# The first feed-forward units of a hybrid decoder step: order of stores, fetches, copies, sums and splits

## The chip, the core and the metric

The kernel runs on one core of a Trainium2 chip. The core has a matrix engine (TensorE, PE in the profile, with its weight loads as PEld), a vector engine (VectorE, DVE), a scalar engine (ScalarE, ACT), GpSimd (POOL) and a sync engine (SyncE, SP) that here only issues DMAs. Each engine works through its own queue in order and waits on semaphores for the others. The metric is the device time of one execution in microseconds: 2213.25 us before the change, the median of three runs (2213.18 to 2215.95).

## What is computed

One inference step of one decoder layer, in float32, for a prompt of 2048 tokens and 64 sample tokens (8 sequences of 8), with a model width of 1024. The mixing half has sliding-window attention and gated linear attention side by side; the feed-forward half, in which the change lies, is this:

```python
mix = jnp.einsum('bte,ed->btd', jnp.concatenate([attn.astype(x.dtype), gla_out], axis=-1), w_out)
x = x + rms_norm(mix, g_mix_post)

h = rms_norm(x, g_ffn_pre)
u = jax.nn.relu(jnp.einsum('btd,df->btf', h, w_up))
f = jnp.einsum('btf,fd->btd', u * u, w_down)
x = x + rms_norm(f, g_ffn_post)
```

with `w_up` of 1024 x 4096 and `w_down` of 4096 x 1024.

## The kernel before

**Splitting into high and low parts.** To get float32 results from a faster format, every operand of a matmul is split in two: ScalarE writes the high part (a copy into `float32r`), VectorE writes the remainder (`source - high`). `split_by` (line 1555) is this pair. A product is then three matmuls per 128 rows of depth: high x high, high x low, low x high.

**Row blocks.** The 2048 tokens are 16 row blocks of 128, and the samples are one more. The output projection goes over them in `B_ORDER` (line 68), which ends with 14, 11, 15. For each row block `residual` (line 1474) adds the residual and normalizes, then eight transposes on TensorE write the result to two PSUM banks, ScalarE copies these into a tile `ht`, and for every second row block of a pair VectorE makes four differences in `ht` and a DMA stores the tile to DRAM, `h_d` (line 1514). `residual` is a generator: each `next` does one part, so that its parts can be placed between other work. `ht` has one slot for all pairs (tag `st` of the pool `keep`), so that a new pair's copies must wait until the store of the pair before has landed. Row block 14's store empties the slot for row block 11's copies. After them, row block 15's copies and its store use the same tile; unit two's result tile takes the slot over from there.

**Units.** The product with `w_up` is computed for each half of the prompt in 16 units of 256 columns (`up`, line 1652). A unit is one level of a Strassen-like scheme: seven products of 12 matmuls, numbered 1 to 7, each of an operand block `H[p]` (kept on chip, in two parts) and of a weight or a sum of weights. In the first half of the prompt there are also two products for the samples (numbered 0 and 8) and two transposes of their result (9). Products 1, 0 use the weight half `a` (`ua`, `ub` in the profile is the bank that a product fills, not the weight); 2, 8, 4 use the half `b` (called w1 here); 5, 7 use the sums `s13`; 6, 3 use the sums `s24`. VectorE makes the sums (`sums_13`, `sums_24`), ScalarE and VectorE split them (`split_sums`) and the weights (`split_up`). VectorE also gathers the products into seven results, ScalarE squares them, and a DMA stores them (`s_d`).

Products 2, 3 and 4 add to the bank that 1, 5 and 7 have filled, so that the earlier value must have been read by then. The bank of 5 and 3 is called Z, that of 7 and 4 V. `uc` is Z's name in the profile, `ud` that of V in unit one, `ua` that of product 6 in unit one and of products 1 and 2 in unit two. `sam` is the sample products' bank; ScalarE's copy of it (`both`) is what the two transposes read.

**Unit one** is special. Its blocks `H[3]` to `H[7]` come from `h_d` by DMA and are split while it runs: blocks 5 and 7 just ahead of it, 6, 3 and 4 within it. `UP_FIRST` (line 49) gives the order of its products: 1, 0, 2, 8, 5, 7, 9, 6, 3, 4. Behind each, `opening` (line 1771) places other work: the parts of row block 15's `residual` (`last_rows`), the blocks' splits, and the sums and splits for unit two. The instructions of this stretch on TensorE, ScalarE and VectorE (`te`, `ac`, `dv`) are chained by the class `InOrder` (line 120) in the order in which the program issues them. DMAs on SP, and row blocks 11 and 14, are ordered by a planner that simulates the program; `tc.issue_after` puts a DMA behind another on SP.

**Memory.** Block 6 comes into a temporary tile in memory that the output projection frees, blocks 3 and 4 into pools in memory that row block 15's tiles free. Blocks 3 and 4 are fetched into the place of their low part and split in place (`split_in_place`). Weights of odd units come into the staging tiles through which block 5 came (`hs_pool`). Down sums (`sum_down`, from unit three on) need pieces of `w_down` that `load_down` fetches into two tiles that held gains before.

Of the kernel before, what the change touches and what calls it, by code (L numbers as in the profile page):

```python
# [21 lines left out]
P = 128  # L22
# [118 lines left out]
def hybrid_step_kernel(ctx: ExitStack, tc: tile.TileContext, I, O):  # L141
# [1330 lines left out]
    gpost = gains(I["g_mix_post"][0], 0, "gpost")  # L1472

    def residual(i, banks, tensor=nc.tensor, scalar=nc.scalar, vector=nc.vector):

# [20 lines left out]
        for h in range(2):  # L1496
            kk = slice(h * 4, h * 4 + 4)
            pt = (bank([P, 512], "ce"[h], f"xnT_{i}_{h}") if te is tensor else next_bank("cdce", f"xnT_{i}_{h}")).rearrange("p (k t) -> p k t", k=4)
            for k in range(4):
                tensor.transpose(pt[:, k, :n], x1[:n, (h * 4 + k) * P : (h * 4 + k + 1) * P], ident[:n, :n])  # L1500
            if i == NB:
                split_copy(xsT[:, kk, :NS], xsT[:, kk, NS:], pt[:, :, :NS], vector)
                continue
            ht = sums[sb, j]
            scalar.activation(ht[:, (6, 2)[h] if second else h], pt, AF.Copy)
            if sb == 0 and not second:
                split_copy(H[h + 1][0][:, :, q], H[h + 1][1][:, :, q], pt, vector)
# [5 lines left out]
        kept = slice(2 * (sb == 0), 7)  # L1513
        nc.sync.dma_start(h_d[sb][:, kept, :, q], ht[:, kept])

    h_raws = {}

    def fetch_h(sb, p, home="h"):
        h_raws[p] = []
        for k in range(0, KT // 2, 2):  # L1520
            if isinstance(home, tuple):
                pool, tag = U[home[k // 2]], "s"
            else:
                pool, tag = {"h": hs_pool, "t": keep}.get(home) or U[home], f"{home}{k // 2}"
            raw = pool.tile([P, 2, BT], F32, tag=tag, name=f"hraw_{sb}_{p}_{k}", bufs=1)
            nc.sync.dma_start(raw, h_d[sb][:, p - 1, k : k + 2])
            h_raws[p].append(raw)

    def load_h(sb, p, scalar=nc.scalar, vector=nc.vector):
# [13 lines left out]
    def load_up(sb, fc):  # L1543
# [8 lines left out]
        for c, raw in enumerate(raws[sb, fc]):  # L1552
            nc.sync.dma_start(raw, src[:, 4 * c : 4 * c + 4])

# [14 lines left out]
    for n, i in enumerate(B_ORDER[2:]):  # L1569
# [25 lines left out]
    fetch_h(0, 7, ("s24h", "s24l"))  # L1595
    fetch_h(0, 6, "tmp")

# [54 lines left out]
    def up(sb, fc, before, steps=iter(())):  # L1652
# [6 lines left out]
        sam = bank([P, BT], "b", f"sam_{fc}") if sb == 0 else None  # L1659
        place = []  # L1660

# [58 lines left out]
        for p in UP_FIRST if first else UP_ORDER:  # L1720
# [37 lines left out]
        add(4, s(5), s(0))  # L1758
        if sb == 0:
            sample_features(fc, sam)  # L1760

# [9 lines left out]
    def opening(p, taken, ahead):  # L1771

        if p == 1:
            taken(p)
        elif p == 0:
            next(last_rows)
        elif p == 2:
            taken(p)
            next(last_rows)
            run(load_h(0, 6, ac, dv))  # L1780
            U.pop("tmp").release()
        elif p == 8:
            taken(p)
            sums_24(0, 0, dv)
            split_sums(0, 0, 24, ac, dv)
        elif p == 5:
            taken(p)
        elif p == 7:
            taken(p)
            next(last_rows)  # L1790
            close_pools(R)
            for q in H_LATE[3:]:
                h_pools[q] = open_pool(f"h_{q}")
            for q in H_LATE[:2:-1]:
                h_place(0, q)
                for k in range(0, KT // 2, 2):
                    loaded = nc.sync.dma_start(f32(H[q][1][:, k : k + 2]), h_d[0][:, q - 1, k : k + 2])
            with tc.issue_after(loaded.ins):
                load_up(0, 2)
        elif p == 9:  # L1800
            taken(p)
        elif p == 6:
            split_in_place(3)
            ahead("a")
            taken(p)
            split_in_place(4)
            run(last_rows)
            for half in range(2):
                load_down(0, half)
        elif p == 3:  # L1810
            ahead("s13")
            ahead("13")
        else:
# [12 lines left out]
    def sample_features(fc, sam):  # L1826
# [3 lines left out]
        ac.activation(sq, turned[:, :, 1], AF.Copy)  # L1830
        dv.tensor_tensor(sq, sq, turned[:, :, 0], op=ALU.add)
        squared(sq)
        split_by(ac, dv, parts[:, :, :NS], parts[:, :, NS:], sq)
# [252 lines left out]
    split_sums(0, 0, 13, ac, dv)  # L2086
    load_up(0, 1)
    next(last_rows)
    run(load_h(0, 7, ac, dv))
    for sb in range(NSB):  # L2090
# [13 lines left out]
        if sb == 0:  # L2104
            for p in (3, 4, 7, 6):
                h_pools.pop(p).release()
# [55 lines left out]
```

## Time and profile before

| | |
|---|---|
| median of 3 runs | 2213.25 us (2213.18 to 2215.95) |
| profiled execution | 2212.31 us |
| its span | 2210.4 us |
| TensorE granted clock, mean | 0.995 |
| HBM traffic | 266.34 MB read, 143.99 MB written |
| weight fetch of a unit (`raw`), issue to landing | 4.4 us for 512 KB |
| result store of a unit (`s_d`), issue to landing | 8.5 us for 1792 KB |

The profile is that of one execution. A row of it names the engine, the line, the operation and the tiles, written one first; most operations of this stretch go through `InOrder` and so show its line, L130, and are told apart by their tiles. Times are microseconds from the start of the span. An idle time is put down to what ended it: `[2.96 <-ACT s L130]` is 2.96 us of idle time that ended with ScalarE's write of a tile `s`. On `SPq` a row is the issue of a DMA, not its transfer. The first unit starts at 893 us and lasts some 30 us, of 2210.

### The profile page before, as it was taken

The page shows a single profiled execution, that of the slowest core. Times are in us where ns is not written, and L with a number is a line of the kernel's source. Part 1 is how long each engine was busy: PE and PEld are TensorE (multiplying, and loading weights), DVE is VectorE, ACT ScalarE, POOL GpSimd, SP SyncE. Part 2 cuts the span into 40 slices and gives each one's busy share as a digit, 9 for nine tenths or more (in the row PEclk, how much of TensorE's full clock was granted, in tenths as well). Part 3 has the DMA queues.
Part 4 walks back from the last instruction along what each step waited for, and adds up shares of the span by engine and source line. Part 5 has one row for each costly group of instructions (what it writes and reads, how often), then busy time and mean ns, then how long its engine had stood idle before and what let it go on. Part 6 is the DMA issues. An engine that isn't in the chain of part 4 may idle for free.

```text
span 2210.4 us, 34115 instructions
## 1 busy us (share of the span) xinstructions
PE 2166.2 (98%) x11784; PEld 1864.2 (84%) x11784; DVE 1530.4 (69%) x3101; ACT 1220.3 (55%) x2626; POOL 262.3 (12%) x418
## 2 busy tenths in 40 slices
PE   8999999999999999899999999999999999999998
PEld 7989989999997788688888887888888888888886
DVE  5888868777785665788888655547776666555566
ACT  5889867566664443555555544435455444454454
POOL 3576512111111010000000000000000000000000
PEclk9999999999999999999999999999999999999999
DMA  7344332224336665768777677768553344666685
GB/s 228 131 143 149 102 104 65 68 80 142 126 125 219 214 217 181 240 226 274 256 271 255 248 228 225 246 187 264 175 204 139 137 154 148 229 203 197 191 271 186
DMA packets 240185, 411.53 MB, mean 186 GB/s; under 512 B 25924, under 2 KB 142124, under 8 KB 235900
## 3 DMA queue, kind: packets, MB, share of 16 engines
q1 hardware_dynamic: 240012, 409.35, 55.8%
q8 instruction: 93, 1.52, 0.3%
q14 instruction: 80, 0.66, 0.1%
HBM read 266.34 MB, written 143.99 MB: 186 GB/s over the span
## 4 chain that ended last, share of the span: by engine, by line
PE 83%; DVE 7%; ACT 5%; DMA 2%; issue 2%; POOL 1%; SPq 0%; DVEq 0%; ACTq 0%; POOLq 0%
PE dn L130 27%; PE gproj L130 9%; PE uc L130 7%; PE ua L130 7%; PE out L1306 6%; PE proj L130 5%; PE ud L130 4%; PE ub L130 4%; PE ue L130 4%; PE sam L130 1%; PE dsam L130 1%; PE av L130 1%; PE o L130 1%; PE pT L130 1%; PE sc L130 1%
## 5 line engine op out<-in xcount | busy, mean ns | idle before, releaser
L130 PE MATMUL dn<-o0t,o0s 128*128 128x512 f32 x896 | 349.1, 390 | 1.7 <-ACT f L1936 1.5
L130 PE MATMUL dn<-o1t,o0s 128*128 128x512 f32 x896 | 349.5, 390 | 0.3 <-DVE o1t L219 0.2
L130 PE MATMUL dn<-o0t,o1s 128*128 128x512 f32 x896 | 349.3, 390 | 0.0
L219 DVE TENSOR_TENSOR o1s<-rs,o0s 128x512 fp32r<-128x512 f32 x224 | 154.6, 691 | 231.0 <-ACT o0s L218 224.8
L218 ACT ACTIVATE o0s<-rs 128x512 fp32r<-128x512 f32 x224 | 141.1, 631 | 306.2 <-PE dn L130 284.0
L130 PE MATMUL gproj<-wg,gxh 128*128 128x384 f32 x1024 | 272.4, 342 | 0.3 <-DVE gp_s L213 0.3
L130 ACT ACTIVATE st<-st 128x512 f32<-128x512 f32 x224 | 141.2, 630 | 141.8 <-DVE st L130 137.8
L130 PEld LDWEIGHTS dn<-o0t,o0s 128*128 128x128 f32 x896 | 168.2, 188 | 38.6 <-ACT f L1936 1.9
L130 PEld LDWEIGHTS dn<-o1t,o0s 128*128 128x128 f32 x896 | 168.2, 188 | 37.1 <-DVE o1t L219 1.1
L130 PEld LDWEIGHTS dn<-o0t,o1s 128*128 128x128 f32 x896 | 168.2, 188 | 35.4
L130 PE MATMUL uc<-H,s 128*128 128x512 f32 x768 | 188.5, 394 | 1.7 <-ACT s L130 1.2
L130 PEld LDWEIGHTS gproj<-wg,gxh 128*128 128x128 f32 x1024 | 183.8, 188 | 4.1 <-issue 3.1
L130 PE MATMUL gproj<-wg,gxl 128*128 128x384 f32 x576 | 186.0, 340 | 0.2 <-DVE gp_s L213 0.2
L130 PE MATMUL ua<-H,w 128*128 128x512 f32 x744 | 179.2, 390 | 0.0
L130 PEld LDWEIGHTS uc<-H,s 128*128 128x128 f32 x768 | 144.2, 189 | 33.2 <-ACT s L130 1.6
L130 PEld LDWEIGHTS ua<-H,w 128*128 128x128 f32 x744 | 139.7, 188 | 29.4
L1306 PE MATMUL out<-wo,mt 128*128 128x512 f32 x680 | 160.4, 394 | 2.6 <-ACT mt L218 1.5
L219 DVE TENSOR_TENSOR o1t<-rt,o0t 128x512 fp32r<-128x512 f32 x224 | 153.3, 684 | 6.7 <-ACT o0t L218 6.7
L208 POOL TENSOR_TENSOR frs<-rs_v,half 128x1 f32<-128x1 f32 (+1 forms) x13 | 10.1, 787 | 1213.5 <-DVE rs_v L206 693.1
L1306 PEld LDWEIGHTS out<-wo,mt 128*128 128x128 f32 x680 | 127.4, 189 | 29.6 <-ACT mt L218 1.9
L218 ACT ACTIVATE o0t<-rt 128x512 fp32r<-128x512 f32 x224 | 138.3, 618 | 6.7 <-PE dn L130 3.1
L130 DVE TENSOR_TENSOR st<-st 128x512 f32<-128x512 f32 x160 | 110.6, 691 | 26.9 <-ACT st L130 22.6
(398 smaller groups left out, 4318.0 us busy)
## 6 DMA issues: line engine op xcount, KB each, us to landing
s_d<-st SPq DMA_DIRECT2D x32, 1792.0 KB, 8.5
rs<-s_d SPq DMA_DIRECT2D x224, 256.0 KB, 3.0
raw<-in_w_up SPq DMA_DIRECT2D x64, 512.0 KB, 4.4
rt<-t_d SPq DMA_DIRECT2D x128, 256.0 KB, 3.9
rt<-in_w_down SPq DMA_DIRECT2D x96, 256.0 KB, 2.8
t<-in_w_down SPq DMA_DIRECT2D x64, 256.0 KB, 3.9
t_d<-t SPq DMA_DIRECT2D x32, 512.0 KB, 3.2
hraw<-h_d SPq DMA_DIRECT2D x20, 512.0 KB, 5.4
```

Of the source, the lines that this page charges most:

```text
L130: ins = call(*a, **k)
L208: nc.gpsimd.tensor_tensor(out, v[:n], e, op=ALU.pow)
L218: nc.scalar.activation(hi, src, AF.Copy)
L219: vector.tensor_tensor(lo, src, f32(hi), op=ALU.subtract)
L1306: te.matmul(banks[c], x, w[:, c * 512 : (c + 1) * 512], start=k + u == 0, stop=k == KT - 1 and u == len(products) - 1,)
```

## The change

Seven things in the stretch around unit one:

1. Row block 14's store is issued behind the fetches of block 6 and of unit two's weights, and those weights behind block 6.
2. Row block 11's copies out of the PSUM banks get a place in ScalarE's fixed order, behind product 2.
3. Block 3 is fetched, behind that store, into four free planes of unit one's result tile, and split from there. Block 4 alone is fetched into the place of its low part.
4. Row block 15's parts come one or two products earlier: its sums behind product 1, its transposes behind product 5 and not behind 7. The last part, differences and store, comes behind product 3 and not behind 6.
5. Block 7's split goes in two: the high parts ahead of unit one, the remainders behind product 1. The sums for `s24` come behind the sample product 0, their split ahead of block 6's.
6. The sums and splits for unit two are spread: weights behind product 2 (were behind 6), `s13` behind 5 and 9 (was behind 3). A first part of the sample features comes behind product 6.
7. The pieces of `w_down` are fetched behind row block 15's store.

```diff
-H_EARLY, H_LATE = (1, 2), (5, 7, 6, 4, 3)
+H_EARLY, H_LATE = (1, 2), (5, 7, 6, 3, 4)
...
-            scalar.activation(ht[:, (6, 2)[h] if second else h], pt, AF.Copy)
+            copy = (ht[:, (6, 2)[h] if second else h], pt, AF.Copy)
+            if i == B_ORDER[-2]:
+                late_copies.append(copy)
+            else:
+                scalar.activation(*copy)
...
-        nc.sync.dma_start(h_d[sb][:, kept, :, q], ht[:, kept])
+        if i == B_ORDER[-3]:
+            yield
+        latest_store[:] = [nc.sync.dma_start(h_d[sb][:, kept, :, q], ht[:, kept])]
...
+    def split_apart(sb, p):
+        h_place(sb, p)
+        parts = [([t[:, 2 * n : 2 * n + 2] for t in H[p]], raw) for n, raw in enumerate(h_raws.pop(p))]
+        for (hi, _), raw in parts:
+            ac.activation(hi, raw, AF.Copy)
+        yield
+        for (hi, lo), raw in parts:
+            dv.tensor_tensor(lo, raw, f32(hi), op=ALU.subtract)
+        yield
...
-        if n != 1:
+        if i == B_ORDER[-1]:
+            waiting_rows = residual(*early.pop(0))
+            run(waiting_rows, 5)
+        elif n != 1:
             run(residual(*early.pop(0)))
...
-    fetch_h(0, 6, "tmp")
+    sixth = fetch_h(0, 6, "tmp").ins
...
+                elif p == 6:
+                    next(features)
...
         if p == 1:
             taken(p)
+            next(last_rows)
+            next(seventh)
         elif p == 0:
             next(last_rows)
+            sums_24(0, 0, dv)
         elif p == 2:
             taken(p)
-            next(last_rows)
+            ahead("a")
+            for copy in late_copies:
+                ac.activation(*copy)
+        elif p == 8:
+            taken(p)
+            split_sums(0, 0, 24, ac, dv)
             run(load_h(0, 6, ac, dv))
             U.pop("tmp").release()
-        elif p == 8:
-            taken(p)
-            sums_24(0, 0, dv)
-            split_sums(0, 0, 24, ac, dv)
         elif p == 5:
-            taken(p)
-        elif p == 7:
             taken(p)
             next(last_rows)
             close_pools(R)
             for q in H_LATE[3:]:
                 h_pools[q] = open_pool(f"h_{q}")
-            for q in H_LATE[:2:-1]:
-                h_place(0, q)
-                for k in range(0, KT // 2, 2):
-                    loaded = nc.sync.dma_start(f32(H[q][1][:, k : k + 2]), h_d[0][:, q - 1, k : k + 2])
+            ahead("s13")
+            run(load_h(0, 3, ac, dv))
+            h_place(0, 4)
+            loaded = None
+            for k in range(0, KT // 2, 2):
+                with tc.issue_after(loaded.ins) if loaded else nullcontext():
+                    loaded = nc.sync.dma_start(f32(H[4][1][:, k : k + 2]), h_d[0][:, 3, k : k + 2])
             with tc.issue_after(loaded.ins):
-                load_up(0, 2)
+                latest_store[:] = [load_up(0, 2)]
+        elif p == 7:
+            taken(p)
+            split_in_place(4)
         elif p == 9:
             taken(p)
+            ahead("13")
         elif p == 6:
-            split_in_place(3)
-            ahead("a")
             taken(p)
-            split_in_place(4)
+        elif p == 3:
             run(last_rows)
-            for half in range(2):
-                load_down(0, half)
-        elif p == 3:
-            ahead("s13")
-            ahead("13")
+            with tc.issue_after(latest_store[0].ins):
+                for half in range(2):
+                    load_down(0, half)
...
-    load_up(0, 1)
+    with tc.issue_after(sixth):
+        second_up = load_up(0, 1)
+    with tc.issue_after(second_up.ins):
+        run(waiting_rows)
+    st_first = U["st0"].tile([P, 7, BT], F32, tag="st", name="st_0_0", bufs=1)
+    h_raws[3] = [st_first[:, 4:6], st_first[:, 2:7:4]]
+    loaded = latest_store[0]
+    for n, raw in enumerate(h_raws[3]):
+        with tc.issue_after(loaded.ins):
+            loaded = nc.sync.dma_start(raw, h_d[0][:, 2, 2 * n : 2 * n + 2])
     next(last_rows)
-    run(load_h(0, 7, ac, dv))
+    seventh = split_apart(0, 7)
+    next(seventh)
```

More of the change, by code (lines that the diff above doesn't have):

```diff
@@ L1 @@
 from collections import deque
-from contextlib import ExitStack
+from contextlib import ExitStack, nullcontext
 from itertools import chain, cycle, islice
@@ L1525, in fetch_h @@
             raw = pool.tile([P, 2, BT], F32, tag=tag, name=f"hraw_{sb}_{p}_{k}", bufs=1)
-            nc.sync.dma_start(raw, h_d[sb][:, p - 1, k : k + 2])
+            fetched = nc.sync.dma_start(raw, h_d[sb][:, p - 1, k : k + 2])
             h_raws[p].append(raw)
+        return fetched
     def load_h(sb, p, scalar=nc.scalar, vector=nc.vector):
@@ L1659, in up @@
         sam = bank([P, BT], "b", f"sam_{fc}") if sb == 0 else None
-        place = []
+        features = sample_features(fc, sam) if sb == 0 else iter(())
+        place = [st_first] if first else []
         def s(n):
@@ L1758, in up @@
         add(4, s(5), s(0))
-        if sb == 0:
-            sample_features(fc, sam)
+        run(features)
         def end():
```

7 lines of the change are left out of this document (5 added, 2 removed).

## The prediction

> **What bounds the kernel now.** I read the page first, then the time windows around the first feed-forward units, then who made TensorE wait there, then the time-ordered rows of TensorE, the SP queue, ScalarE and VectorE.
>
> ```profile
> span 2210.4 us, 34115 instructions
> PE 2166.2 (98%) x11784; PEld 1864.2 (84%) x11784; DVE 1530.4 (69%) x3101; ACT 1220.3 (55%) x2626; POOL 262.3 (12%) x418
> ```
>
> TensorE is busy for 98% of the span, so only its idle time and its slow stretches can be won. In the windows the columns are length, busy time of PE, PEld, DVE, ACT, POOL, granted clock, DMA share, GB/s.
>
> ```profile
> 893.32:951.36 58.04, 49.98 (x215) 39.24 (x213) 42.62 (x54) 31.08 (x47) 1.95 (x2) 0.91 0.72 234
> 951.36:972.65 21.29, 21.29 (x104) 17.85 (x102) 18.27 (x30) 11.77 (x21) 0.00 (x0) 1.00 0.57 199
> 895.00:900.00 5.00, 5.00 (x27) 4.26 (x26) 4.97 (x6) 0.91 (x2) 1.41 (x1) 1.00 1.09 344
> 920.80:924.00 3.20, 1.90 (x7) 1.36 (x8) 2.68 (x3) 1.44 (x2) 0.00 (x0) 1.00 0.00 0
> 927.60:930.90 3.30, 1.60 (x7) 0.70 (x6) 2.14 (x3) 2.21 (x3) 0.00 (x0) 1.00 0.96 285
> 931.00:934.30 3.30, 3.30 (x10) 2.53 (x9) 2.08 (x4) 1.22 (x2) 0.00 (x0) 0.50 0.95 255
> ```
>
> The first row is units one and two, the second is unit three, which runs undisturbed in 21.29 us. Two such units and the 0.8 us of transposes inside the first (their row below has 1.03, of which 0.2 overlaps what follows) would take 43.4; the chip took 58.0. So 14.7 us is all that the change can win here: 9.8 before unit two starts at 925.23 (925.23 - 893.32 - 21.29 - 0.8), 4.8 behind it. The waits and the rows where they lie:
>
> ```profile
> PE ua L130 <- ACT s L130: 3.0, 1, 3.0
> PE sam L130 <- ACT both L130: 1.3, 2, 0.7
> PE ud L130 <- ACT H L130: 1.3, 1, 1.3
> PE uc L130 <- ACT s L130: 1.2, 1, 1.2
> PE ud L130 <- DVE H L130: 0.8, 1, 0.8
> PE uc L130 <- DVE s L130: 0.5, 1, 0.5
> ```
> ```profile
> 903.59 2.88 PE L130 MATMUL ud<-H,s 128*128 128x512 f32 x12
> 906.32 1.03 PE L130 MATMUL xnT<-ident,x 128*128 128x128 f32 x8
> 907.92 0.44 PE L130 MATMUL sam<-ident,both 128*128 128x128 f32 x2 [0.57 <-ACT both L130]
> 911.32 5.89 PE L130 MATMUL ua<-H,s 128*128 128x512 f32 x12 [2.96 <-ACT s L130]
> 925.23 2.88 PE L130 MATMUL ua<-H,w 128*128 128x512 f32 x12
> 930.54 4.14 PE L130 MATMUL uc<-H,s 128*128 128x512 f32 x10 [0.52 <-DVE s L130]
> 940.99 1.11 PE L130 MATMUL sam<-w,xsT 128*128 128x256 f32 x8
> ```
>
> The waits sum to 8.1; the rest is clock. Twelve matmuls (one product) show 2.88 and pass in 2.75 (903.59 to the transposes behind them); those at 911.32 show 5.89. The windows tell why: a stretch with PE busy for 1.60 of 3.30 is followed by 3.3 us at half clock, one with 1.90 of 3.20 is not.
>
> The Trainium skill has another rule ("TensorE: Matmul & The Clock Gate", section "Why this matters for your kernels"): the clock falls after an idle gap of about 3 us. Here it fell after gaps of 1.2 and 0.5 us. By the page the 1.0 us of clock in the second unit below would not come and the losses would sum to 8.7, not 9.7; I go by the rows.
>
> **The store moves behind four fetches.**
>
> ```profile
> 890.22 2.12 SPq L1553 DMA_DIRECT2D raw<-in_w_up  x2
> 892.43 0.78 SPq L1526 DMA_DIRECT2D hraw<-h_d  x1
> 894.89 0.53 SPq L1514 DMA_DIRECT2D h_d<-ht  x1
> 895.47 5.65 SPq L1526 DMA_DIRECT2D hraw<-h_d  x1
> 908.88 1.75 SPq L1797 DMA_DIRECT2D H<-h_d  x4
> 926.40 0.57 SPq L1514 DMA_DIRECT2D h_d<-ht  x1
> ```
> ```profile
> h_d<-ht SPq DMA_DIRECT2D x3, 1792.0 KB, 8.5
> raw<-in_w_up SPq DMA_DIRECT2D x8, 512.0 KB, 4.2
> H<-h_d SPq DMA_DIRECT2D x4, 512.0 KB, 5.8
> ```
> ```profile
> 903.44 1.09 ACT L1505 ACTIVATE ht<-xnT 128x512 f32<-128x512 f32 x2
> 906.54 1.06 ACT L130 ACTIVATE H<-hraw 128x1024 fp32r<-128x1024 f32 x1 [2.01 <-DMA hraw<-h_d]
> 907.50 0.37 ACT L130 ACTIVATE both<-sam 128x256 f32<-128x256 f32 x1
> 907.63 1.23 DVE L130 TENSOR_TENSOR H<-hraw,H 128x1024 fp32r<-128x1024 f32 x1 [3.01 <-ACT H L130]
> 902.11 1.28 DVE L130 SCALAR_TENSOR_TENSOR x<-bx,bssq,gpre 128x1024 f32<-128x1024 f32 x1 [0.66 <-POOL bssq L208]
> 895.29 1.41 POOL L208 TENSOR_TENSOR bssq<-rs_v,half 128x1 f32<-128x1 f32 x1 [8.76 <-DVE rs_v L130]
> ```
>
> Now the second half of block 6 (895.47) stands behind the store of row block 14 (894.89); ScalarE gets it at 906.54, and the sums, the split and the ua product follow late. After the change both halves go first, then the two weight fetches that went at 890.22, then the store. The first fetch is free no sooner than now, 893.2. Up to the store's last byte the queue moves 4 x 512 + 1792 KB, 3.93 MB, 11.4 us at 344 GB/s: 904.6 at the earliest. At the latest it lands now's 903.4 (894.89 + 8.5) plus a block fetch (1.5) plus the weights' lost head start (3.0): 907.9. I take 906.3, between the two, since bytes start and land some time after issue.
>
> **The bank copies get a fixed place on ScalarE.** The copies of row block 11 write the slot that this store empties: now they start at 903.44, the moment it lands, and harm nothing, for ScalarE's next input comes at 906.54 anyway. After the change they stand at one place of a fixed queue, behind product 2's squares and the weights' split (done near 902.5), and start at 906.3; behind them wait the sample copy, the split of the second sums (s24), both halves of block 6, everything later on ScalarE, and VectorE after it. TensorE waits too: row block 15's transposes, moved ahead of product 7, write the same two banks. It reaches them at 903.59, where product 5 ends and product 7 starts now. First copy done 906.9, second 0.5 later: product 7 starts at 908.0, not at 904.4 (903.59 + 0.8): **3.6 lost**. The input of the transposes (902.11 + 1.28 = 903.4) is ready by then: its chain gains up to 0.9 on POOL (1.41 against about 0.5) and gets 2.4 of block 7's remainders put before it; that wait covers it. Were it gone, 0 to 1 us would show. The idle stretch of 3.5 halves the clock for one stretch of 3.4: ten matmuls at 930.54 show 4.14 where 2.4 would do (ten twelfths of 2.88), **1.7 lost**. It is two stretches at most, 3.4, and none at the least.
>
> **Sums, splits and third block, first unit.** ScalarE's fixed order from 907.4 on: sample copy (0.4) to 907.8, s24 (1.0) to 908.8, block 6's two halves (2.0) to 910.8, the copies of Z and of row block 15 (1.6) to 912.4, block 3 (2.0) to 914.4. VectorE follows each with a remainder of 1.2: s24 at 909.9, block 6 at 911.1 and 912.1, then the sums for unit two (1.2) and block 3 at 915.6. TensorE has product 7 from 908.0 to 912.4 (2.75 + 1.7), the two sample transposes, the ua product from 912.6 to 915.3, and product 3 needs block 3's second half half-way, at 916.7. Everything is there before it is asked for, by 0.8 to 2.7 us: so the waits of 0.57 and 2.96 and ua's slow clock go, and the 1.3 and 0.8 before product 4 with them. Block 3's two fetches, in the idle staging tile, land some 3 us behind the store, 909.3, and ScalarE asks at 912. The x1 store goes behind them (512 KB, 1.5 more); if block 3's home is the memory it reads, that is 910.8, still in time. Block 4 still waits for VectorE's end with block 6 (now 908.88 after 907.63 + 1.23): 912.1, and lands 4 to 6 later, its first remainder at 918.4 for a product due at 918.0: **0.2**, 0 to 2. Of the 9.8, 5.5 stays; unit two starts at 920.9.
>
> **Second unit.** The early split for its sums (VectorE done near 920) takes away 1.2, 0.5 and their clock. Late next is VectorE's backlog.
>
> ```profile
> L130 DVE TENSOR_TENSOR s<-t,s 128x1024 fp32r<-128x1024 f32 x6 | 7.3, 1223 | 4.7 <-ACT s L130 4.7
> L130 DVE TENSOR_TENSOR st<-st 128x512 f32<-128x512 f32 x6 | 4.1, 690 | 0.2
> L130 DVE TENSOR_TENSOR ht<-ht 128x512 f32<-128x512 f32 x4 | 2.7, 688 | 0.1
> ```
> ```profile
> 939.78 0.58 ACT L130 ACTIVATE st<-ua 128x512 f32<-128x512 f32 x1
> ```
>
> From 912.1 it has, before the remainder that the second sample product (now at 940.99) needs: seven of about 1.15 (blocks 3 and 4, two splits of sums, that remainder), sixteen of 0.6 to 0.7 (four sums, eight adds, row block 15's four), 0.5 of sample work: 19, and some 3.2 of waiting for ScalarE's squares and splits: 934.3. TensorE gets there at 932.8 (920.9 + four products and a sample product of 0.95): **1.5 lost**, 0.5 to 2 if a wait of ScalarE comes out longer or shorter. Then half clock, or instead, as products run on, a wait for the sample copy behind the same backlog: **1.7**; both, where the stretch of 3.4 us that the clock goes by happens to begin badly, **1.0** on average. That is 4.2 here, 3.2 to 4.9 by these cases, for 4.8 now.
>
> VectorE's 18.27 of 21.29 in unit three leaves it room, and the down sums' weights, now after row block 15's store (926.40 + 8.5), come some ten us before the first down sums in unit three: 0. Their four DMAs no longer stand ahead of block 3's fetches on SP; POOL has nothing in its queue but the two powers of row block 15.
>
> **Sum.** Lost now 14.7, after 5.5 + 4.2 = 9.7: 5.0 won. Behind unit three nothing changes, and TensorE's idle time there is small, so the gain stays. The profiled execution took 2212.31 (2210.4 and 1.9 around), 0.9 under the median 2213.25; so 2207.3 as that one, 2208.3 as a median. What this kernel's measurement can tell from nothing is about 0.2%, 4.4 us.
>
> **Rivals.**
> (a) The store lands at 904.6, or the copies are not held by it. Lost before product 7 is then 1.9 or less, the clock may hold, VectorE's backlog starts earlier: 2 to 4 us more, 2205.5. For it: nothing but fetches stands ahead of the store. Against: the copies at 903.44 started just as it landed.
> (b) The gain is eaten: it lands at 907.9, which shifts the chain on ScalarE and VectorE by 1.6, and the clock takes 0.9 more: 2.5 won, 2211. For it: the clock rows; the 3.0 head start that the weights lose.
> (c) Slower: SP becomes the bound. The queue is held for 5.65 behind a 1792 KB store, and block 3, the x1 store, block 4 and the next weights now stand there. Losses pass 19.1 when the store and what follows come 9 us later than reckoned (landing past 915.5): then 2218 and more. Against: the next issue was held for 5.65 only, and no later store stands before 926.40. The same would follow if row block 15's store, which empties unit two's result slot (first written at 939.78, wanted near 934), landed past 943.
>
> **How the numbers follow.** My forecast 0.38, (a) 0.16, (b) 0.32, (c) 0.14. The forecast's cases reach from 2206.5 to 2209.5; with (a), (b) and the near end of (c) the range is 2203.5 to 2215.5, leaving out gains over 10 and most of (c). Over 0.2% faster: most of the forecast and (a), 0.50; within: (b) and the rest, 0.37; slower: 0.13.
>
> **What would show it.** Right: TensorE idle near 903.6 for about 3.5 us before the transposes, released by ScalarE's bank copy, which starts as the store lands near 906; half clock behind it; no wait at the ua product, little at products 3 and 4; unit two near 921; a wait for VectorE's w1 remainder at the second sample product; unit three near 946.5 for 951.36. Wrong: no wait before the transposes (a), or waits on fetches of block 3 or 4 (c).

## The result, and the profile after

The changed kernel takes 2208.41 us (median of 14 runs, 2204.73 to 2211.96), the kernel before, run beside it, 2213.36 (14 runs, 2210.11 to 2215.95). The ratio is 0.9977, its 95% interval 0.9969 to 0.9985: 5.0 us faster, with 2208.3 predicted. The profiled execution took 2205.27, 7.0 below the profiled one of before; it is the second fastest of the 14 runs, so that its 7.0 is more than the runs in general show. The first lines of its page:

```profile
span 2203.4 us, 34114 instructions
PE 2162.3 (98%) x11784; PEld 1862.3 (85%) x11784; DVE 1531.6 (70%) x3101; ACT 1219.9 (55%) x2626; POOL 261.7 (12%) x418
```

The time windows of both units, then of each, then of unit three (columns as before: start and end, length, busy time of PE, PEld, DVE, ACT, POOL, granted clock, DMA share, GB/s):

```profile
892.52:943.57 51.05, 45.72 (x215) 36.27 (x214) 42.28 (x54) 31.08 (x48) 1.09 (x2) 1.00 0.78 255
892.52:918.08 25.56, 23.45 (x114) 18.53 (x112) 22.01 (x26) 16.66 (x24) 1.09 (x2) 1.00 0.86 275
918.08:943.57 25.49, 22.27 (x103) 17.74 (x102) 20.27 (x29) 14.42 (x24) 0.00 (x0) 1.00 0.71 235
943.57:964.86 21.29, 21.29 (x104) 17.85 (x102) 18.29 (x30) 11.77 (x21) 0.00 (x0) 1.00 0.64 219
```

The two units take 51.05 where they took 58.04. TensorE's idle time (length less PE busy) fell from 8.06 to 5.33, by 2.7; its busy time fell from 49.98 to 45.72, by 4.3, for the same 215 matmuls, because the clock is 1.00 where it was 0.91. So most of the profiled gain is clock. The runs say so too: each run's record has its mean granted clock, and the mean is 0.9969 over the 19 runs of the changed kernel in this series and the next, and 0.9952 over the 27 runs of the kernel before in the next; 0.0017 of 2210 us is 3.8 us.

Who made TensorE wait, and its rows in order of time:

```profile
PE sam L130 <- DVE w L130: 1.3, 1, 1.3
PE uc L130 <- ACT st L130: 1.1, 1, 1.1
PE uc L130 <- DVE H L130: 0.8, 1, 0.8
PE ud L130 <- DVE H L130: 0.8, 1, 0.8
PE sam L130 <- ACT both L130: 0.7, 1, 0.7
PE xnT L130 <- ACT ht L130: 0.6, 1, 0.6
```
```profile
903.50 1.14 PE L130 MATMUL xnT<-ident,x 128*128 128x128 f32 x8 [0.56 <-ACT ht L130]
907.38 2.99 PE L130 MATMUL ua<-H,s 128*128 128x512 f32 x12
911.37 2.80 PE L130 MATMUL uc<-H,s 128*128 128x512 f32 x11 [0.76 <-DVE H L130]
915.45 2.79 PE L130 MATMUL ud<-H,w 128*128 128x512 f32 x11 [0.76 <-DVE H L130]
931.97 1.10 PE L130 MATMUL sam<-w,xsT 128*128 128x256 f32 x7 [1.32 <-DVE w L130]
934.14 3.03 PE L130 MATMUL uc<-H,s 128*128 128x512 f32 x12 [1.08 <-ACT st L130]
```

The wait of 2.96 at the ua product and the 1.28 before product 4 are gone. Six waits of 0.56 to 1.32 stand in place of seven up to 2.96, and none of them brings half clock here. The SP queue and ScalarE around the store:

```profile
884.39 5.80 SPq L1534 DMA_DIRECT2D hraw<-h_d  x4
890.28 1.27 SPq L1572 DMA_DIRECT2D raw<-in_w_up  x2
894.10 0.53 SPq L1522 DMA_DIRECT2D h_d<-ht  x1
894.73 6.85 SPq L2127 DMA_DIRECT2D st<-h_d  x2
901.66 0.42 SPq L1400 DMA_DIRECT2D x_d<-bx  x1
```
```profile
902.85 1.09 ACT L130 ACTIVATE ht<-xnT 128x512 f32<-128x512 f32 x2 [1.36 <-DMA h_d<-ht]
908.99 2.01 ACT L130 ACTIVATE H<-st 128x1024 fp32r<-128x1024 f32 x2 [0.48 <-DMA x_d<-bx]
913.08 1.06 ACT L130 ACTIVATE H<-H 128x1024 fp32r<-128x1024 f32 x1 [2.08 <-DMA H<-h_d]
933.00 0.60 ACT L130 ACTIVATE st<-ua 128x512 f32<-128x512 f32 x1 [0.90 <-DMA h_d<-ht]
```

All four fetches of blocks 7 and 6 are issued by 890.19, the store at 894.10, and the bank copies start as it lands at 902.85: 10.3 after the first product, as before (903.44 - 893.32 = 10.1). Now block 6 waits for ScalarE, not the reverse.

### The profile page after: what moved, and what is told of

Same layout as the page of the kernel before. It is cut to its first block, busy times and chain, and to the rows that moved or that the text cites. A ratio compares the mean times of both kernels' runs of the same rounds, so it can differ in the third digit from the quotient of the medians.

```text
span 2203.4 us, 34114 instructions
## 1 busy us (share of the span) xinstructions
PE 2162.3 (98%) x11784; PEld 1862.3 (85%) x11784; DVE 1531.6 (70%) x3101; ACT 1219.9 (55%) x2626; POOL 261.7 (12%) x418
## 4 chain that ended last, share of the span: by engine, by line
PE 84%; DVE 7%; ACT 4%; DMA 2%; issue 1%; POOL 1%; SPq 0%; DVEq 0%; ACTq 0%; POOLq 0%
PE dn L130 27%; PE gproj L130 9%; PE uc L130 7%; PE ua L130 7%; PE out L1306 6%; PE proj L130 5%; PE ud L130 4%; PE ue L130 4%; PE ub L130 4%; PE sam L130 1%; PE dsam L130 1%; PE av L130 1%; PE o L130 1%; PE pT L130 1%; PE sc L130 1%
## 5 line engine op out<-in xcount | busy, mean ns | idle before, releaser
L208 POOL TENSOR_TENSOR frs<-rs_v,half 128x1 f32<-128x1 f32 (+1 forms) x13 | 10.1, 787 | 1208.0 <-DVE rs_v L206 687.9
L218 ACT ACTIVATE o0t<-rt 128x512 fp32r<-128x512 f32 x224 | 138.3, 618 | 11.1 <-DMA rt<-t_d 8.2
```

What stands on the lines that cost most here:

```text
L208: nc.gpsimd.tensor_tensor(out, v[:n], e, op=ALU.pow)
L218: nc.scalar.activation(hi, src, AF.Copy)
```

## Experiments

The table has, for every kernel run, the median, its difference to the kernel before in the same series and that ratio's interval, and from its profile the length from the first product to unit three, TensorE's idle time in it (length less PE busy) and the granted clock there. The profile is of one execution, the median of 5 to 14. The changed kernel itself came out at -5.0 in one series and at -7.1, with five runs, in the next; so a difference of about 2 us between two kernels is not told by their medians. It ran in these two series alone, and kernels of later series are compared with it by their difference to the kernel before.

| kernel | us | to before | ratio, 95% | two units | idle | clock |
|---|---|---|---|---|---|---|
| before | 2213.4 to 2214.1 | | | 58.04 | 8.06 | 0.91 |
| changed | 2208.41 | -5.0 | 0.9969 to 0.9985 | 51.05 | 5.33 | 1.00 |
| after_again | 2206.96 | -7.1 | 0.9953 to 0.9978 | 50.91 | 5.16 | 1.00 |
| a_store_between | 2209.19 | -4.9 | 0.9969 to 0.9986 | 52.58 | 5.48 | 0.97 |
| a_sums_late | 2211.43 | -2.6 | 0.9981 to 0.9998 | 56.16 | 7.72 | 0.94 |
| a_block3_in_place | 2208.53 | -5.1 | 0.9969 to 0.9987 | 51.16 | 5.33 | 1.00 |
| a_copies_free | 2206.27 | -7.3 | 0.9954 to 0.9978 | 50.73 | 4.53 | 0.93 |
| b_store_behind | 2212.61 | -1.5 | 0.9983 to 1.0001 | 57.13 | 8.81 | 0.97 |
| b_sums_early | 2211.93 | -1.8 | 0.9984 to 1.0001 | 56.18 | 7.59 | 0.94 |
| b_three_moves | 2208.01 | -5.9 | 0.9966 to 0.9986 | 52.29 | 4.51 | 0.93 |
| a_not_held | 2204.70 | -9.0 | 0.9954 to 0.9979 | 50.90 | 5.14 | 1.00 |
| a_diff_early | 2205.49 | -8.1 | 0.9949 to 0.9977 | 49.59 | 4.11 | 1.00 |
| a_diff_swap_x1 | 2204.76 | -8.8 | 0.9947 to 0.9972 | 48.61 | 3.52 | 1.00 |
| a_all | 2203.81 | -9.9 | 0.9943 to 0.9970 | 47.73 | 3.03 | 1.00 |

### The changed kernel once more

> The changed kernel once more, for a second profile of it. Its profiled execution took 2205.27, its median is 2208.41, while the same pair before is 2212.31 and 2213.36. Theory A (the order of the work has no chance in it, the clock has): the waits come back to within 0.2 us (1.3 at the sample product, 1.1, 0.8, 0.8, 0.7, 0.6), and a slower execution shows stretches of 3.4 us at half clock somewhere, each 1.7 us; a median of 2208 means about two more of them than the profile of 2205.27 has. Theory B (landing times of DMAs differ between executions): the waits around the store of row block 14 and at the products 3 and 4 change by over 1 us.

Its windows, unit one and unit two:

```profile
891.03:916.46 25.43, 23.44 (x114) 18.52 (x112) 21.91 (x26) 16.67 (x24) 1.08 (x2) 1.00 0.87 274
916.46:941.94 25.48, 22.31 (x104) 17.74 (x102) 20.25 (x29) 14.42 (x24) 0.00 (x0) 1.00 0.71 232
```

Both units agree with the first profile to 0.13 us, and the waits to 0.3 (product 3 waits 0.48 for 0.76). The order has little chance in it, as theory A has it. That slower executions have more stretches at half clock no profile shows, since both profiled ones were fast; but the 19 runs of this kernel go with their mean clocks: four at 0.998 have a mean of 2205.4 us, ten at 0.997 one of 2208.1, four at 0.996 one of 2209.8, and the one at 0.995 took 2209.8. The five runs here have a median of 2206.96, 1.6 above the profiled execution; in the first series the distance was 3.1.

### One part undone at a time

**a_store_between**: the first part undone.

```diff
-        if i == B_ORDER[-3]:
-            yield
...
-    with tc.issue_after(sixth):
-        second_up = load_up(0, 1)
-    with tc.issue_after(second_up.ins):
-        run(waiting_rows)
+    load_up(0, 1)
...
```

> The changed kernel with the first part undone alone: the store of row block 14 stands between the two fetches of block 6 again, and unit two's weights ahead of them. Theory S (the first unit's gain is the store's place): block 6's second half is held behind the store as it was, lands near 905.5, ScalarE takes it at 905.5 to 906.5, the product of block 6 (ua) waits 2 to 3 us again and half clock follows; 4 to 6 us slower than the changed kernel, 2212 to 2214. Theory U (the gain is the early sums and splits for unit two and the earlier s24): ua waits less than 1 us and the time stays within 1.5 us of the changed kernel, 2207 to 2210.

Its SP queue, then windows of 3.41 us in its second unit:

```profile
890.12 2.12 SPq L1570 DMA_DIRECT2D raw<-in_w_up  x2
892.33 0.46 SPq L1532 DMA_DIRECT2D hraw<-h_d  x1
894.80 0.53 SPq L1520 DMA_DIRECT2D h_d<-ht  x1
895.38 6.70 SPq L1532 DMA_DIRECT2D hraw<-h_d  x1
```
```profile
932.84:936.25 3.41, 1.71 (x10) 1.43 (x11) 3.09 (x5) 2.44 (x5) 0.00 (x0) 1.00 1.02 292
936.25:939.66 3.41, 3.41 (x10) 2.64 (x9) 3.01 (x4) 1.37 (x2) 0.00 (x0) 0.50 1.04 314
```

Theory S falls. The queue is that of before, block 6's second half is held for 6.70 again, and yet ua does not wait at all: TensorE waits 1.0 longer before the transposes (1.57), since the store lands later, and block 6's split has always stood behind the copies in this kernel. That 1.0 is given back later (TensorE's idle time is 5.48 for 5.33 in all), and the 1.5 us more that the units take are the one stretch at half clock. The time is 2.2 above that of the changed kernel in the same series, a little more than theory U's 1.5; but to the kernel before it is -4.9, where the changed kernel has -5.0 and -7.1, so that no cost of this edit is clear of the noise.

**a_sums_late**: the sixth part undone.

```diff
         elif p == 2:
-            ahead("a")
...
         elif p == 5:
-            ahead("s13")
...
         elif p == 9:
-            ahead("13")
         elif p == 6:
+            ahead("a")
             taken(p)
         elif p == 3:
+            ahead("s13")
+            ahead("13")
```

> The changed kernel with the sums and splits for unit two back at their old places: the weights behind product 6, the sums s13 and their split behind product 3. Theory S (the first unit carries the gain): unit two starts no later, or up to 1.5 us earlier because VectorE has less to do ahead of blocks 3 and 4; waits of 1.2 and 0.5 for ScalarE's and VectorE's part of s13 come back in the second unit, and the time is 0 to 2 us above the changed kernel, 2208.4 to 2210.4. Theory U: 3 to 5 us slower, 2211.4 to 2213.4.

Its waits of TensorE:

```profile
PE uc L130 <- ACT s L130: 2.9, 1, 2.9
PE xnT L130 <- ACT ht L130: 2.2, 1, 2.2
```

4.5 us above the changed kernel in the same series, theory U's 3 to 5, and 2.4 above it by the difference to before of the first series. Unit two's second product waits 2.9 for the split of s13 (1.2 and 0.5 for both its parts before the change), and half clock follows. Part of the profile's loss is not this edit: its store took 10.40 us to land (894.92 to 905.32) where the changed kernel's took 8.75, hence the 2.2; and the profiled execution, 2214.63, is the slowest of the eleven.

**a_block3_in_place**: the third part undone; block 3 fetched like block 4.

```diff
-    h_raws[3] = [st_first[:, 4:6], st_first[:, 2:7:4]]
...
-            run(load_h(0, 3, ac, dv))
-            h_place(0, 4)
+            for q in (3, 4):
+                h_place(0, q)
...
+            split_in_place(3)
```

> The changed kernel with its third part undone alone: block 3 is fetched into the place of its low part, as block 4 is, and so only when row block 15's x1 store and transposes are done with that memory. Theory F (the early fetch of block 3 carries product 3): its fetch is issued near 907 or later and lands 4 us behind, ScalarE takes it near 911.5 for 909.0, product 3 waits 2 to 3 us more, block 4 comes 1.5 later, half clock may follow; 2 to 4.5 us slower than the changed kernel. Rival (the fetches were quick enough before): within 1 us.

Theory F falls: 51.16 us for the two units, the waits before products 3 and 4 are 0.45 and 0.76, as in the changed kernel. With no fetch of block 3 behind the store, the x1 store of row block 15 goes out sooner and frees the memory sooner:

```profile
897.14 3.00 SPq L1400 DMA_DIRECT2D x_d<-bx  x1
904.49 4.83 SPq L1827 DMA_DIRECT2D H<-h_d  x4
```

Block 3 is fetched at 904.49 and ScalarE has it at 908.29 without a wait. The third part is worth nothing that the profile shows.

**a_copies_free**: the second part undone.

```diff
-            if i == B_ORDER[-2]:
-                late_copies.append(copy)
-            else:
-                scalar.activation(*copy)
+            scalar.activation(*copy)
```

> The changed kernel with its second part undone alone: row block 11's copies have no fixed place on ScalarE; the planner puts them behind block 6's split and the copy of Z instead of behind the weights' split. Theory H (the place matters, since row block 15's transposes wait for these copies and now stand ahead of product 7): the copies come 3.5 to 4 us later (the sample copy, the split s24, block 6 and Z's copy take 4.1 of ScalarE), TensorE idles 3.5 to 4.5 before the transposes, half clock follows, and the copy of Z waits for nothing; 3 to 6 us slower than the changed kernel. Rival (the copies wait for the store's landing anyway, so their place is worth little): within 1 us.

Its waits of TensorE in both units, and its windows: the stretch before the slow ones, the slow ones, unit one, unit two.

```profile
PE xnT L130 <- ACT ht L1508: 4.4, 1, 4.4
```
```profile
899.39:902.80 3.41, 1.27 (x6) 0.73 (x4) 3.38 (x5) 1.79 (x3) 0.00 (x0) 1.00 0.86 200
902.80:909.63 6.83, 4.57 (x15) 3.99 (x16) 5.07 (x6) 5.84 (x10) 0.00 (x0) 0.50 0.78 269
...
890.24:919.36 29.12, 24.72 (x114) 20.50 (x112) 24.20 (x30) 18.57 (x28) 1.08 (x2) 0.88 0.75 238
919.36:940.97 21.61, 21.48 (x103) 17.76 (x102) 17.93 (x25) 12.61 (x21) 0.00 (x0) 1.00 0.84 275
```

This is the run that tells most. The wait came as theory H says, 4.4 us with two stretches of half clock behind it, and unit one lasts 29.12, 3.6 longer. And the time is no worse, 2206.27 (-7.3 to before, for -5.0 and -7.1), and the two units take 50.73 together: unit two loses 0.3 where it lost 4.2. VectorE shows why. Here is its split of the w1 remainder, first in the changed kernel, then in this one:

```profile
930.69 1.22 DVE L130 TENSOR_TENSOR w<-raw,w 128x1024 fp32r<-128x1024 f32 x1
```
```profile
928.10 1.22 DVE L130 TENSOR_TENSOR w<-raw,w 128x1024 fp32r<-128x1024 f32 x1
```

It starts 38.2 us after the first product there (892.52) and 37.9 here (890.24). So VectorE keeps its pace, TensorE comes to unit two 3.6 later, and the later waits vanish. The losses of the two units are not two terms but one account.

### Parts put into the kernel before

**b_store_behind**: the store alone.

```diff
...
+    with tc.issue_after(sixth):
+        run(waiting_rows)
     next(last_rows)
...
```

> The kernel before with one thing changed: the store of row block 14 is issued behind both fetches of block 6; all else stays. Theory S: block 6's second half lands near 897 instead of 906, the waits of 2.96 (ua) and its slow clock go; what stays is the 0.57 at the transposes of the sample result, the waits before product 4 and the second unit: 4 to 6 us faster than before, 2207 to 2209, so about all of the change's gain. Theory U: 0 to 1.5 us faster, 2212 to 2213, since the waits before product 4 and in the second unit take the time instead.

Rows of SP, ScalarE and TensorE, a fence for each:

```profile
895.13 0.53 SPq L1516 DMA_DIRECT2D h_d<-ht  x1
```
```profile
906.79 1.09 ACT L1505 ACTIVATE ht<-xnT 128x512 f32<-128x512 f32 x2 [2.24 <-DMA h_d<-ht]
```
```profile
920.64 0.50 PE L130 MATMUL ud<-H,w 128*128 128x512 f32 x1 [3.15 <-ACT H L130]
```

The 2.96 at ua falls to 0.87 in two parts, as theory S has it, and the time gains 1.5 only, theory U's, with an interval that reaches 1.0001: product 4 now waits 3.15 for block 4's split, which stands on ScalarE behind product 6's squares.

**b_sums_early**: the early sums alone.

```diff
         elif p == 5:
             taken(p)
+            ahead("a")
+            ahead("s13")
...
         elif p == 9:
             taken(p)
+            ahead("13")
...
```

> The kernel before with the sums and splits for unit two at their new time alone: weights and sums s13 behind product 5, the split of s13 behind the sample transposes; store, copies, blocks 3 and 4, row block 15's parts and w_down as they were. Theory E (the early sums carry the gain, as taking them out of the changed kernel lost 3 to 4.5 us): the waits of 1.2 and 0.5 at unit two's second product go and half clock behind them; 3 to 4.5 us faster than before, 2209.5 to 2211. Theory P (no part carries it alone; whichever comes late on VectorE takes the time): VectorE has 4.5 us more to do before blocks 3 and 4, product 4 waits 1 to 3 us more, and the gain is under 1.5 us, 2212 to 2214.

Gain 1.8, and again the interval reaches 1.0001. The waits of unit two's second product are gone, the one at ua (3.0) stays, and products 3 and 4 wait 1.4 each, which product 3 did not do before. Theory P comes nearer than E, though product 4, which waited 2.0 before, waits less and not more: alone, each move shows the next late thing.

**b_three_moves**: both, and block 4's split ahead of product 6's squares.

```diff
...
             split_in_place(3)
-            ahead("a")
-            taken(p)
             split_in_place(4)
+            taken(p)
...
```

> The kernel before with three moves and nothing else: the store of row block 14 behind both fetches of block 6; the sums and splits for unit two early (weights and s13 behind product 5, the split of s13 behind the sample transposes); block 4's split on ScalarE ahead of product 6's squares, which it stood behind. The first two gave 1.5 and 1.8 us alone. Theory C (each takes away one lateness of several on the same chain, so each alone only shows the next one, and together they give about the change's gain): the waits of 2.96 at ua, 1.2 and 0.5 at uc in the second unit and 3.1 at product 4 are all under 1.3, the two units take 51 to 53 us, at most one stretch at half clock, and the time is 4.5 to 7 us below before, 2206.5 to 2209. Rival A (the moves add up and no more): 3 to 3.5 us, 2210 to 2211. Rival R (the rest of the change carries it: the fixed place of the copies, block 3 in unused staging, row block 15's parts sooner): under 3 us, the units take 55 us or more.

Its windows (unit one, unit two):

```profile
892.90:923.90 31.00, 26.49 (x113) 20.46 (x112) 26.12 (x32) 17.57 (x26) 1.95 (x2) 0.89 0.82 264
923.90:945.19 21.29, 21.29 (x104) 17.85 (x102) 16.37 (x24) 13.55 (x23) 0.00 (x0) 1.00 0.79 252
```

5.9 us faster than before, in theory C's range, above A's 3.5: three moves like those of the change, put into the kernel before, give about what the whole change gives (5.0 and 7.1 in its two series). The third was not run alone, nor the first two without it; so rival A, which puts it at nothing, falls only if that move by itself gives clearly less than 2.6 us. Theory C was wrong in the detail: product 3 still waits 2.7 (2.07 for ScalarE, 0.65 for VectorE), two stretches at half clock follow, and then unit two runs undisturbed, in 21.29. Again a loss in the first unit and none in the second.

### The waits that are left

**a_diff_early**: row block 15's differences and store behind product 6.

```diff
         elif p == 6:
             taken(p)
-        elif p == 3:
             run(last_rows)
...
```

> The changed kernel with row block 15's last part (its four differences on VectorE, its store and the fetches of w_down behind it) issued behind product 6 instead of product 3. In the changed kernel VectorE idles for 1.53 just before the differences (it waits for ScalarE's samq, which waits behind the squares). Theory V (VectorE's backlog sets the second unit's waits): the differences fill that idle time, all that follows on VectorE comes about 1.5 us sooner, the remainder that the second sample product waits for is ready before it is asked for (1.3 goes to about 0), row block 15's store starts 2 us sooner, ScalarE's wait of 0.9 for the slot goes and the 1.1 at uc and the 0.7 at the sample transposes shrink; 1.5 to 3 us faster than the changed kernel, unit three 1.5 to 3 us sooner after unit two. Theory W (the waits are ScalarE's order and come back elsewhere): under 0.7 us.

The wait for the w1 remainder (1.3) is gone, that for the slot is 0.3 for 1.1, the one for the sample copy 1.5 for 0.7: 49.59 for the units, 1.4 less than the two profiles of the changed kernel. Filling 1.5 us of VectorE's idle time gave 1.4 in the profile, just under theory V's 1.5 to 3, which had the wait for the sample copy shrink and not grow.

**a_diff_swap_x1**: the same, the x1 store between block 3's fetches, the homes of blocks 3 and 4 swapped.

```diff
-H_EARLY, H_LATE = (1, 2), (5, 7, 6, 3, 4)
+H_EARLY, H_LATE = (1, 2), (5, 7, 6, 4, 3)
...
             next(last_rows)
+            with tc.issue_after(x1_store[0].ins):
+                nc.sync.dma_start(h_raws[3][1], h_d[0][:, 2, 2:4])
             next(seventh)
...
```

> The same, and beside it row block 15's x1 store is issued between the two fetches of block 3 instead of behind both, and the homes of blocks 3 and 4 are swapped, so that block 4's fetch waits for that store and no longer for VectorE's end with block 6. Theory V: the x1 store lands about 1 us sooner (near 907.7 where it was 908.9), ScalarE's wait of 0.48 before block 3 goes, block 4's fetch goes about 1 us sooner, its wait of 2.08 on ScalarE falls to 1 and product 4's wait of 0.76 goes; 0.5 to 1.2 us faster than without it, unit two starts 0.5 to 1.2 us sooner after the first product. Rival: the two waits before products 3 and 4 stay, since VectorE and not the fetch orders them; 0 to 0.3.

Product 4 no longer waits, unit one is 24.85 for 25.70, and the units 48.61: 1.0 less, as theory V has it. Block 4 comes to ScalarE 18.6 us after the first product, for 20.6 in the changed kernel. The medians of the two, 2205.49 and 2204.76, are too close to tell apart.

**a_not_held**: copies behind block 6's first half, transposes behind product 7.

```diff
         elif p == 2:
-            for copy in late_copies:
-                ac.activation(*copy)
...
-            run(load_h(0, 6, ac, dv))
+            block6 = load_h(0, 6, ac, dv)
+            next(block6)
+            for copy in late_copies:
+                ac.activation(*copy)
+            run(block6)
...
         elif p == 5:
             taken(p)
+        elif p == 7:
+            taken(p)
             next(last_rows)
...
```

> The changed kernel with nothing on ScalarE held by the store of row block 14: row block 11's copies stand behind the split s24 and the first half of block 6, and row block 15's transposes behind product 7 (with them the sums s13 of unit two, block 3's split and block 4's fetch). Theory B (units one and two share one budget, VectorE's chain: 42 us of work in 51, and TensorE's waits are where it catches up): with the copies behind other work ScalarE's idle time of 1.4 before them goes, TensorE's wait of 0.6 at the transposes goes, product 6 waits at most 0.5 for block 6's remainder, and the two units take 49.3 to 50.3 instead of 51.0; 0.7 to 1.7 us faster than the changed kernel. Rival (each wait has its own cause): the second unit's waits of 1.3, 1.1 and 0.7 stay to 0.1, the first unit alone gains 0.5 or less.

The rival is right: 50.90, the second unit's waits stay at 1.3, 1.1 and 0.7, and what the transposes gain (0.3 for 0.6) product 3 loses (1.3 for 0.8), since block 3's split came later. Its five runs have a low median, 2204.70, but reach 2210.78; their mean is 2206.2, and the profile shows no reason for a gain over the changed kernel.

**a_all**: the last two together.

> The same together with the differences behind product 6, the x1 store ahead and the homes of blocks 3 and 4 swapped. Theory B: the gains add up, since each takes idle time out of VectorE's chain: the two units take 47.0 to 48.2 us (48.6 with the last three alone), and the time is 0.4 to 1.6 us below that kernel, 2203 to 2204.5, the fastest here. Rival: the transposes, 3 us later, bring row block 15's differences and store back to where they were, the wait of 1.5 for the sample copy in unit two grows by what the first unit gains, and the sum stays at 48.6 or above.

```profile
893.71:918.12 24.41, 22.88 (x113) 18.60 (x112) 22.37 (x27) 16.54 (x24) 1.08 (x2) 1.00 0.90 288
918.12:941.44 23.32, 21.82 (x104) 17.83 (x102) 19.52 (x28) 14.46 (x24) 0.00 (x0) 1.00 0.82 269
```

47.73, 3.2 us less than in the changed kernel, and 2203.81, the fastest here: 9.9 below before, 0.9957 (0.9943 to 0.9970). It beats the kernel before clearly. Against the changed kernel the intervals overlap; the profile's 3.2 us is the firmer evidence. Here the transposes' new place seems to help, by 0.9 (47.73 for 48.61); but in the profile of a_diff_swap_x1 the store also landed 0.8 later than in the changed kernel (11.1 after the first product for 10.3), which may be part of it.

## Why the prediction was right, and where it was not

The number (2208.3 for 2208.41), the sign and the size of the gain were right. Its working was right in part, and two errors cancelled: that the median was met to 0.1 us is luck.

**The store.** The step "the first fetch is free no sooner than now, 893.2" failed, and with it 904.6 as the earliest landing. The row of 892.43 was put down to a wait for TensorE, but the fetch stood behind the two weight fetches on SP, which end their issue at 892.34 (890.22 + 2.12). In a_store_between the weights stand ahead again, and the fetch again comes right behind them (890.12 + 2.12 = 892.24, then 892.33); in the changed kernel, with nothing ahead, block 6's fetches are out by 890.19. So all fetches went 3 to 4 us sooner than reckoned and did not delay the store: it was issued 1.58 after the first product, as before (1.57), landed at 902.85 and not at 906.3, and the 3.6 before the transposes came out as 0.56. The mechanism was rival (a)'s, which had 0.16.

**Half clock in the first unit**, 1.7 predicted: none in two profiles, since the idle stretch that was to cause it did not come. Where it did come (a_copies_free, 4.4), half clock followed, as the rule taken from the trace says.

**Products 3 and 4**, "0" and "0.2": 0.76 each. TensorE came sooner than reckoned and blocks 3 and 4 did not: block 3 was held 0.48 by the x1 store, block 4's fetch by VectorE's end with block 6, as the prediction said. First unit: 3.47 lost (918.08 - 892.52 - 21.29 - 0.8) for 5.5. Of this 2.1 is waits; the other 1.4 is busy time above that of undisturbed products (23.45 for 22.09), for which the prediction had no term.

**Second unit**, 4.2 predicted: 4.20 (943.57 - 918.08 - 21.29), and 4.19 in the second profile. The wait for the w1 remainder is 1.32 for 1.5. The rest is not what was reckoned: 1.08 for row block 15's store in unit two's result slot, which the prediction had only as a way to a loss (rival (c)), 0.67 for the sample copy, and about 1.0 of products that took longer than in unit three (22.27 busy for 21.29), perhaps since their operands came just in time, which no run here separates. The sum for VectorE held: from its end with block 6 (908.69) to the end of that remainder (931.91) it took 23.2, with 22.2 reckoned, and since TensorE came sooner as well, their distance, the wait, was about as forecast. Half clock, reckoned at 1.0 on average, came behind these same waits in one of five profiles (the changed kernel twice, a_store_between, a_block3_in_place, a_not_held).

**The sum.** 7.7 lost for 9.7, so 7.0 won between the profiles for 5.0. That the median came out as predicted is the second error: it lies 3.1 above the profiled execution in the first series (0.9 was reckoned from the kernel before) and 1.6 in the second.

**What the terms left out.** The sum treats the units' losses as terms that add. a_copies_free, with the 3.6 us wait realized and more, and b_three_moves show that they do not: the second unit's loss depends on how far VectorE and ScalarE are behind when TensorE gets there. What the second unit would have lost with the store landed at 906.3 no run shows: the wait for it would have held ScalarE, and VectorE behind it, too, which a_copies_free does not do.

**Which part carries the gain.** Not one: the store alone gives 1.5 and the early sums 1.8, neither clear of nothing, and both with block 4's split 5.9. Undone alone, the sums cost 4.5 against the five runs of their series (2.4 by the first series); the store's place, block 3's fetch and the copies' place cost nothing that can be told. What the earlier parts of row block 15 and of block 7 are worth by themselves was not tried.

## What to carry to other kernels

Before a row's named releaser is used as a bound, look at what stands ahead of it on its own queue: an issue that follows the one before by 0.1 us was waiting for its turn, and will move when the order does. Waits in successive stages that one slow chain feeds are one account, so a wait removed or added early is partly given back later; price the chain (here VectorE, busy 42 of 51 us), and fill its idle time. And a wait can cost the clock besides itself, and not only a long one: waits of 1.2 and 0.5 close together brought 1.7 us of it in the kernel before.

## What the runs showed of the hardware

The clock goes by stretches of 3.41 us. In the rows above, a stretch with PE busy for 1.71 of 3.41 is followed by 0.50, as is one with 1.27. In the changed kernel the two stretches on its own grid that hold the second unit's waits are busier, and the next one is not slowed:

```profile
929.64:933.05 3.41, 2.09 (x12) 1.47 (x11) 3.19 (x6) 1.30 (x3) 0.00 (x0) 1.00 0.94 254
933.05:936.47 3.42, 2.34 (x11) 1.95 (x11) 2.92 (x5) 3.05 (x4) 0.00 (x0) 1.00 1.08 355
936.47:939.88 3.41, 3.41 (x16) 2.48 (x14) 3.34 (x5) 0.91 (x2) 0.00 (x0) 1.00 1.06 356
```

So the same pair of waits (1.3 and 1.1) costs 1.7 us more in a_store_between, where half of the first and all of the second fall into one stretch, and nothing where they fall into two. But how long PE is busy in a stretch does not decide alone. In b_store_behind one with 1.53, less than the 1.71 above, was followed by a stretch at full clock, and only the next one by half clock (922.79 to 926.20 at 0.50):

```profile
915.96:919.37 3.41, 1.53 (x7) 0.94 (x5) 2.33 (x3) 0.98 (x2) 0.00 (x0) 1.00 0.81 254
919.37:922.79 3.42, 1.39 (x5) 0.93 (x6) 2.17 (x2) 2.17 (x3) 0.00 (x0) 1.00 0.01 2
```

What else decides stays open. The Trainium skill ("TensorE: Matmul & The Clock Gate", section "Part 1: The HAM clock gate") has a free-running window of 3413 ns, with which the lengths agree; that an idle window is needed for the fall, as its table puts it, does not agree with a window that is half busy.

The landing of one and the same 1792 KB store varied: 8.75 us from issue to the copy that waits for it in the changed kernel, 10.40 in a_sums_late, 11.66 in b_store_behind (895.13 to 906.79). It goes with the bytes that the DMA engines moved in that time, 2.9, 3.3 and 3.8 MB by the rates in these three stretches (336, 320 and 328 GB/s): in b_store_behind both fetches of block 6 and the weights were issued from 890.45 on, in the changed kernel block 6's were out by 890.19. Why more was under way in a_sums_late stays open. And the issue right behind it is held on SP: 5.65 us in the kernel before, 6.70 in a_store_between, both times a fetch for which the profile shows no other wait.
